# Passing the hi and lo parts of the activations as one moving operand, with weight blocks of 256 columns, in a two-layer encoder trunk

## The chip, the cores and the metric

The kernel runs on one core of one Trainium2 chip. The metric is the device time of one execution in microseconds; the median of three runs before the change is 2806.14 us (2806.04 to 2807.89). Engines are named as in the profile: PE is TensorE's matmul, PEld its weight load, DVE VectorE, ACT ScalarE, POOL GpSimd, SP SyncE, whose queue issues the DMAs.

## What is computed

A trunk of two layers on 256 tokens of 2048 features, all in float32. The reference, cut to what matters here:

```
for layer in range(2):
    sh1, sc1, g1, sh2, sc2, g2 = split(silu(c) @ mod_w[layer] + mod_b[layer], 6)
    h = rms_norm(x, norm_mix_w[layer]) * (1 + sc1) + sh1
    if layer == 0:                       # gated DeltaNet heads and band attention
        mix = gdn_attn_mixer(h, ab_w_in, ..., ab_w_out)
    else:                                # Mamba-2 SSD: in 2048 -> 10304, out 4096 -> 2048
        mix = mamba2_ssd(h, ssd_w_in, ..., ssd_w_out)
    x = x + g1 * mix
    h = rms_norm(x, norm_mlp_w[layer]) * (1 + sc2) + sh2
    x = x + g2 * (square(relu(h @ mlp_w1[layer])) @ mlp_w2[layer])   # 2048 -> 8192 -> 2048
```

## The kernel before

**Products.** A float32 product is made of three products in float32r. Each operand is split into hi (the float32r rounding) and lo (the rest): weights W into wh and wl, activations into ah and al, and the sum is wh·ah + wh·al + wl·ah. Activations are kept as units, a hi tile and a lo tile of [128, 4 k-tiles, 256 tokens] each. Weights stream through in chunks of 1 MB: 4 k-tiles (512 rows of W) by 512 columns. `loader` (L436) loads a chunk by a DMA on SP's queue into one of 4 raw buffers and splits each half of it: ACT casts wh (L289), DVE subtracts to wl (L290).

`b_item` (L459) makes the products of a chunk feature-major: for each of 4 column tiles and each k-tile three matmuls, each with its own 128x128 weight load and 256 moving columns (tokens):

```
self.mmx(o, wh[:, k, cs], ah[:, ka], st, False)
self.mmx(o, wh[:, k, cs], al[:, ka], False, False)
self.mmx(o, wl[:, k, cs], ah[:, ka], False, sp)
```

I call these three a triple; a chunk has 16. `a_item` (L486) is token-major: the activations are the weights of the array and 512 columns of W move. Matmuls of both come from one helper line, L280.

**PSUM.** The pool `psg` has 4 tiles of one bank. A block of 512 output columns takes two of them, each [128, 2, 256] with two column tiles, and is summed over 4 chunks (K = 2048). `room` (L164) lets a new block begin only when at most one older one still waits for its evacuation.

**Who uses what.** The first mixer's input projection (w_ab) mixes a_items and b_items. b_blocks make: the first mixer's output projection (`out_blocks`, wo_ab, 16 chunks), both MLPs (w1 and w2, 128 chunks a layer), the SSD input projection but for z (48 of 80 chunks of w_ssd; the 32 of z are a_items, `a_block`), and the SSD output projection (wo_ssd, 2 halves of 16 chunks).

**Evacuation.** `residual` (L670): for each column tile one DVE scalar_tensor_tensor, x += g·psum (L677). `relu2` in `mlp` (L1209): for each two column tiles ACT relu (L1214) and square (L1215), then the split by ACT and DVE. `conv` (L684): ACT copies PSUM to a padded buffer (L693) and starts the result (L703), DVE adds three taps a column tile (L709). `ssd_gate` (L1159), `gdn_z` (L934), `norm_unit` (L630) and `split_unit` (L594) write the (hi, lo) units; in `ssd_gate` the last steps are transposes on PE, ACT for hi (L1196) and DVE for lo (L1197).

**Order.** Work is traced in steps: a chunk's products yield four times, and between, `tick` traces steps of waiting evacuations (`fast`), of the mixers' background tasks (`bg`) and of the adaLN modulation (`pump`, DVE products of 2.3 us at L402 on 1 MB loads). Each engine then has its instructions in an order by these priorities and by readiness, fixed when the kernel is built. A chunk is loaded one item ahead of its products. At a layer's norm, `norm` (L652) traces the first two units at once and leaves the others to `fast`. `out_blocks` (L573) takes the last unit's products of its first two blocks after all others of these: that unit is first needed after six chunks.

Of the kernel before, what the change touches and what calls it, by code (L numbers as in the profile page):

```python
# [10 lines left out]
F32 = mybir.dt.float32  # L11
# [14 lines left out]
# blocks of 512 columns of the input projections  # L26
# [3 lines left out]
# columns of the packed vectors  # L30
# [9 lines left out]
class Task:  # L40
    """a generator that traces a piece of work step by step"""
# [34 lines left out]

class Slot:
    """stands for a task to come"""
# [12 lines left out]
class Item:  # L91
    """the products of one weight chunk, in two halves"""
# [5 lines left out]
class Trunk:  # L98
    """Float32 products run as three single-pass float32r products of operands
    split exactly into hi + lo; activations are kept as (hi, lo) units  # L100
    [128, 4 k-tiles, 256 tokens], weights stream through in chunks of
    [128, 4 k-tiles, 512 columns]. The products of the mixers are traced in
    steps between those of the projections."""

    def __init__(self, tc, ctx, ins, out):
# [9 lines left out]
        self.ps_g = pool("psg", 4, space=PSUM)  # L115
# [32 lines left out]
    def pg(self, shape=None):  # L148
        return self.ps_g.tile(shape or [P, 2, SEQ], F32, tag="g", name=self.nm("pg"))

# [6 lines left out]
    def evac(self, gen, frees=10000):  # L157
        """a task that frees a block's PSUM with its first steps"""
# [5 lines left out]
    def room(self):  # L164
        """at most one block in PSUM waits when another begins"""
# [59 lines left out]
    def drain(self, src=None):  # L225
        """all the products up to here; the next chunk's load may go before"""
# [8 lines left out]
    def rsqrt(self, v, n, tag="rs"):  # L235
        """1/sqrt(v) of a [128, n] tile of positive values, by Newton steps."""
# [13 lines left out]
    def softplus(self, v, n, tag):  # L250
        """max(v, 0) + log1p(exp(-|v|)), log1p(u) = 2 atanh(u / (2 + u))."""
# [18 lines left out]
    def priority(self, d):  # L270
        """trace as if d instructions later"""
# [23 lines left out]
    def bc(self, col, n=P):  # L295
        """[128, k] -> [128, k, n] by broadcast"""
# [6 lines left out]
    def constants(self):  # L303
# [13 lines left out]
        # silu(c) along the free axis of every partition  # L317
# [46 lines left out]
        # blocks below the diagonal that join pairs of s-blocks  # L364
# [8 lines left out]
        # the pairs of single rows, transposed  # L373
# [8 lines left out]
    def mod_start(self, layer):  # L382
        """the vectors of a layer, in the order of their use"""
# [32 lines left out]
    def need(self, v, key):  # L416
        """the rest of a modulation vector"""
# [8 lines left out]
    def pump(self, n=None):  # L426
        """as many half chunks of the modulation as are due"""
# [8 lines left out]
    def loader(self, src, whole=False):  # L436
        """loads a packed chunk; gives [(hi, lo)] for its two pairs of k-tiles"""
# [6 lines left out]
        def load():  # L444
            raw = self.raw_p.tile([P, 4, 512], F32, tag="raw", name=self.nm("raw"))
            nc.sync.dma_start(raw.rearrange("p k c -> p (k c)"), src)
            for hf in range(2):
                if whole:
# [1041 lines left out]
```

## Time and profile before

| | |
|---|---|
| median of 3 runs | 2806.14 us |
| lowest, highest | 2806.04, 2807.89 us |
| profiled execution, span (first to last instruction) | 2810.5 us |
| profiled execution, own time beside the span | not listed; the span is used |
| mean granted TensorE clock | 0.994 |
| instructions | 50778, of them 21300 matmuls |

The profile is one execution, apart from the three runs. Busy time is the time in which an engine had an instruction under way; matmuls overlap, so their mean duration (284 ns for 256 columns) is not the distance from one to the next, which is read from start times in the timeline. A row of the chain of waits gives a piece of the path that ended last; a row of the table by stretches gives each engine's busy time and count in that stretch.

### The profile page before, as it was taken

The page shows a single profiled execution, that of the slowest core. Times are in us where ns is not written, and L with a number is a line of the kernel's source. Part 1 is how long each engine was busy: PE and PEld are TensorE (multiplying, and loading weights), DVE is VectorE, ACT ScalarE, POOL GpSimd, SP SyncE. Part 2 cuts the span into 40 slices and gives each one's busy share as a digit, 9 for nine tenths or more (in the row PEclk, how much of TensorE's full clock was granted, in tenths as well). Part 3 has the DMA queues.
Part 4 walks back from the last instruction along what each step waited for, and adds up shares of the span by engine and source line. Part 5 has one row for each costly group of instructions (what it writes and reads, how often), then busy time and mean ns, then how long its engine had stood idle before and what let it go on. Part 6 is the DMA issues. An engine that isn't in the chain of part 4 may idle for free.

```text
span 2810.5 us, 50778 instructions
## 1 busy us (share of the span) xinstructions
PE 2750.8 (98%) x21300; PEld 2661.0 (95%) x21300; DVE 2008.5 (71%) x2820; ACT 1354.7 (48%) x2033; POOL 23.2 (1%) x96
## 2 busy tenths in 40 slices
PE   5999999999999999999999999999999999999999
PEld 5887989999999999999998899988999999999999
DVE  7898898887766666666888976888774444445454
ACT  3444454444344354454568644676445344354442
POOL 1000000000000000000000000000000000000000
PEclk9999999999999999999999999999999999999999
DMA  9895487868877777776565666656655555555553
GB/s 347 330 331 219 165 314 258 303 246 340 307 288 275 270 270 273 277 277 238 209 228 193 247 242 241 223 189 245 241 185 199 187 180 180 182 186 187 180 188 128
DMA packets 96517, 672.32 MB, mean 239 GB/s; under 512 B 12576, under 2 KB 13600, under 8 KB 15392
## 3 DMA queue, kind: packets, MB, share of 16 engines
q1 hardware_dynamic: 96144, 669.07, 65.0%
q8 instruction: 167, 2.74, 0.4%
q14 instruction: 62, 0.51, 0.1%
q10 hardware_dynamic: 144, 0.01, 0.0%
HBM read 666.94 MB, written 2.10 MB: 238 GB/s over the span
## 4 chain that ended last, share of the span: by engine, by line
PE 93%; DVE 5%; ACT 1%; issue 1%; DMA 0%; SPq 0%; DVEq 0%; ACTq 0%
PE pg L280 85%; PE pm L283 4%; PE pm L280 3%; PE pm L286 1%; DVE wl L290 1%; DVE mraw L402 1%; DVE hf L643 0%; DVE u L645 0%; DVE u L1294 0%; DMA mraw<-in_mod_dram 0%; ACT pm L767 0%; DMA x<-in_x_dram 0%; ACT wh L289 0%; ACT u L644 0%; ACT pg L969 0%
## 5 line engine op out<-in xcount | busy, mean ns | idle before, releaser
L280 PE MATMUL pg<-u,wh 128*128 128x256 f32 x11936 | 2165.1, 284 | 3.6 <-ACT u L644 3.4
L280 PEld LDWEIGHTS pg<-u,wh 128*128 128x128 f32 x11936 | 1867.8, 192 | 8.4 <-ACT u L644 4.6
L280 PE MATMUL pg<-u,wl 128*128 128x256 f32 x5968 | 1690.3, 284 | 3.3 <-DVE wl L290 3.2
L290 DVE TENSOR_TENSOR wl<-raw,wh 128x1024 fp32r<-128x1024 f32 x870 | 1059.6, 1223 | 647.3 <-ACT wh L289 642.7
L289 ACT CAST wh<-raw 128x1024 fp32r<-128x1024 f32 x870 | 907.4, 1048 | 1141.1 <-PE pg L280 995.1
L280 PEld LDWEIGHTS pg<-u,wl 128*128 128x128 f32 x5968 | 1146.8, 192 | 5.6 <-DVE wl L290 5.3
L402 DVE SCALAR_TENSOR_TENSOR mraw<-mraw,crow 128x2048 f32<-128x2048 f32 x192 | 438.6, 2285 | 15.9 <-DMA mraw<-in_mod_dram 15.8
L280 PE MATMUL pg<-wh,u 128*128 128x512 f32 x864 | 282.4, 398 | 0.0
L280 PEld LDWEIGHTS pg<-wh,u 128*128 128x128 f32 x864 | 161.5, 188 | 32.6 <-issue 1.0
L280 PE MATMUL pg<-wl,u 128*128 128x512 f32 x432 | 170.3, 394 | 0.5 <-DVE wl L290 0.3
L280 PEld LDWEIGHTS pg<-wl,u 128*128 128x128 f32 x432 | 81.3, 188 | 18.2 <-DVE wl L290 2.2
L709 DVE SCALAR_TENSOR_TENSOR u<-pad,cst,u 128x256 f32<-128x256 f32 x216 | 92.6, 479 | 2.1 <-ACT u L703 1.3
L677 DVE SCALAR_TENSOR_TENSOR x<-pg,mod,x 128x256 f32<-128x256 f32 x176 | 73.6, 477 | 16.6 <-PE pg L280 16.6
L290 DVE TENSOR_TENSOR u<-rl,u 128x512 fp32r<-128x512 f32 x64 | 44.1, 691 | 45.6 <-ACT u L289 45.5
L280 PE MATMUL pm<-u,wh 128*128 128x256 f32 x256 | 49.0, 295 | 19.5 <-ACT wh L289 19.5
L280 PEld LDWEIGHTS pm<-u,wh 128*128 128x128 f32 x256 | 42.2, 204 | 20.5 <-ACT wh L289 20.3
L644 ACT ACTIVATE u<-hf,mod 128x256 fp32r<-128x256 f32 x64 | 29.6, 502 | 63.0 <-DVE hf L643 63.0
L1214 ACT ACTIVATE rl<-pg 128x512 f32<-128x512 f32 x64 | 38.0, 595 | 30.3 <-PE pg L280 30.3
L1215 ACT ACTIVATE rl<-rl 128x512 f32<-128x512 f32 x64 | 40.5, 632 | 1.9
L1103 ACT ACTIVATE sau<-Umask,sd_Ah 128x128 fp32r<-128x128 f32 x128 | 41.0, 403 | 0.0
L1103 ACT ACTIVATE sau<-Umask,sd_Al 128x128 fp32r<-128x128 f32 x128 | 40.9, 401 | 0.0
L289 ACT CAST u<-rl 128x512 fp32r<-128x512 f32 x64 | 39.7, 620 | 2.0
(266 smaller groups left out, 1306.2 us busy)
## 6 DMA issues: line engine op xcount, KB each, us to landing
raw<-in_w_dram SPq DMA_DIRECT2D x256, 1024.0 KB, 4.8
mraw<-in_mod_dram SPq DMA_DIRECT2D x192, 1024.0 KB, 5.1
raw<-in_w_ssd_dram SPq DMA_DIRECT2D x80, 1024.0 KB, 4.8
raw<-in_w_ab_dram SPq DMA_DIRECT2D x56, 1024.0 KB, 5.3
raw<-in_wo_ssd_dram SPq DMA_DIRECT2D x32, 1024.0 KB, 4.8
raw<-in_wo_ab_dram SPq DMA_DIRECT2D x16, 1024.0 KB, 5.2
x<-in_x_dram SPq DMA_DIRECT2D x4, 512.0 KB, 5.1
out_dram<-x SPq DMA_DIRECT2D x8, 256.0 KB, 2.0
```

What stands on the lines that cost most here:

```text
L280: self.nc.tensor.matmul(o, a, b, start=start, stop=stop, skip_group_check=True)
L283: self.nc.tensor.matmul(o, lhsT, rhs, start=True, stop=True, skip_group_check=True)
L286: self.nc.tensor.transpose(o, a, self.ident[:k, :k])
L289: a = self.nc.scalar.copy(hi, src)
L290: b = self.nc.vector.tensor_tensor(lo, src, hi.bitcast(F32), op=ALU.subtract)
L402: x = nc.vector.scalar_tensor_tensor(raw, raw, 1.0, self.crow, op0=ALU.mult, op1=ALU.mult, accum_out=t[:, f : f + 1])
L644: nc.scalar.activation(hi[:, ff], h[:, f], AF.Identity, bias=shift[:, col])
L677: nc.vector.scalar_tensor_tensor(x[:, ff], ps[b][:, f], g[:, cb * 4 + ff : cb * 4 + ff + 1], x[:, ff], op0=ALU.mult, op1=ALU.add)
L709: nc.vector.scalar_tensor_tensor(h, pad[:, f, 1 + q : 257 + q], w[:, q, j : j + 1], h, op0=ALU.mult, op1=ALU.add)
L1103: nc.scalar.activation(au[:, h], self.U, AF.Copy, scale=A[:, t, hd : hd + 1].bitcast(F32))
L1214: nc.scalar.activation(rl, ps[b], AF.Relu)
L1215: nc.scalar.activation(rl, rl, AF.Square)
```

## The change

hi and lo lie side by side: a unit is now a pair of tiles [128, 2 k-tiles, 2 (hi, lo), 256]. A new `c_item` runs one matmul of 512 moving columns (hi and lo) for wh and one of 256 (hi) for wl; the latter is added to the lo columns, so that a column tile has two sums in its bank, [hi·wh | lo·wh + hi·wl], and the evacuation adds them. Chunks for it hold 8 k-tiles by 256 columns (1 MB as before); a block is 256 columns, two chunks for K = 2048. `psg` becomes 2 tiles of two banks. The first mixer's input projection and the SSD's z keep `b_item` and `a_item` (on halves of the new PSUM tiles). Core of the diff:

```diff
-        self.ps_g = pool("psg", 4, space=PSUM)
+        self.ps_g = pool("psg", 2, space=PSUM)
...
+    def pair(self):
+        return [self.unit(F32R, [P, 2, 2, SEQ]) for _ in range(2)]
...
+    def pw(self):
+        return self.ps_g.tile([P, 2, 2, SEQ], F32, tag="g", name=self.nm("pw"))
...
+    def c_item(self, ps, src, act, first, last, after=None):
+        load, ws = self.loader(src)
+        def run():
+            o_ = ps()
+            for hf, (wh, wl) in enumerate(self.tiles(ws, 256)):
+                for ct in range(2):
+                    o = o_[:, ct]
+                    cs = slice(ct * P, ct * P + P)
+                    for k in range(4):
+                        u = act(2 * hf + k // 2)[:, k % 2]
+                        st = first and hf == k == 0
+                        sp = last and hf == 1 and k == 3
+                        self.mmx(o.rearrange("p a t -> p (a t)"), wh[:, k, cs], u.rearrange("p a t -> p (a t)"), st, sp)
+                        self.mmx(o[:, 1], wl[:, k, cs], u[:, 0], False, sp)
+                    yield
...
+    def c_blocks(self, w, cbs, acts, then, r0=0):
...
+        for r in range(2):
+            for cb in cbs:
+                after = (lambda cb=cb: then(ps[cb], cb)) if r else None
+                self.c_item((lambda cb=cb: get(cb)), w[r0 + r, cb], (lambda n, r=r: acts(4 * r + n)), r == 0, r == 1, after)
...
-        seq = [(cb, n) for cb in (0, 1) for n in order[:3]] + [(0, order[3]), (1, order[3])]
-        seq += [(cb, n) for cb in (2, 3) for n in order]
+        seq = [(0, 0), (1, 0), (0, 1), (1, 1)] + [(cb, r) for cb in range(2, 8) for r in range(2)]
...
     def residual(self, ps, cb, key, last, final=False):
...
+        g, x, b = self.mod[2, key], self.x[cb // 2], cb % 2
+        for f in range(2):
+            for n in range(2):
+                nc.vector.scalar_tensor_tensor(x[:, 2 * b + f], ps[:, f, n], g[:, 2 * cb + f : 2 * cb + f + 1], x[:, 2 * b + f], op0=ALU.mult, op1=ALU.add)
...
+    def conv_wide(self, ps, dst, b, tiles, w, bias):
...
+        nc.scalar.copy(th, ps[:, :, 1])
+        nc.vector.tensor_tensor(pad[:, :, 4:], ps[:, :, 0], th, op=ALU.add)
+        for f in range(2):
+            j = tiles + 2 * b + f
+            nc.scalar.activation(dst[:, 2 * b + f], pad[:, f, 4:], AF.Identity, scale=w[:, 3, j : j + 1], bias=bias[:, j : j + 1])
...
         def relu2(ps):
-            hi, lo = self.unit(F32R), self.unit(F32R)
...
+            p = self.unit(F32R, [P, 2, 2, SEQ])
+            lo = self.s2([P, 2, SEQ], tag="rs")
+            nc.scalar.copy(lo, ps[:, :, 1])
+            nc.vector.tensor_tensor(lo, ps[:, :, 0], lo, op=ALU.add)
+            yield
+            rl = self.s2([P, 2, SEQ], tag="rl")
+            nc.scalar.activation(rl, lo, AF.Relu)
+            nc.scalar.activation(rl, rl, AF.Square)
+            self.split(rl, p[:, :, 0], p[:, :, 1])
...
-            for cb in range(4):
-                self.b_block(w1, f * 4 + cb, acts, lambda ps, a=a: a.append(self.evac(relu2(ps))))
+            for cbs in ((f * 8, f * 8 + 1), *((f * 8 + cb,) for cb in range(2, 8))):
+                self.c_blocks(w1, cbs, half, lambda ps, cb, a=a: a.append(self.evac(relu2(ps), 1)))
```

The first two blocks of each w1 group, and of the first SSD block, have their chunks interleaved (`cbs` with two entries). `norm` gives out a unit on demand, tracing it to its end if it isn't yet. The packing on the host follows: w1, w2, wo_ab, wo_ssd and the non-z part of w_ssd in chunks of 256 columns, z of w_ssd as an input of its own.

## Rows read from the trace of the kernel before

**Rows 1.** The profile page's head, its busy times by engine (busy us, share of the span, instructions) and its chain of work that ended last, by engine and by line.

```profile
span 2810.5 us, 50778 instructions
...
PE 2750.8 (98%) x21300; PEld 2661.0 (95%) x21300; DVE 2008.5 (71%) x2820; ACT 1354.7 (48%) x2033; POOL 23.2 (1%) x96
...
PE 93%; DVE 5%; ACT 1%; issue 1%; DMA 0%; SPq 0%; DVEq 0%; ACTq 0%
PE pg L280 85%; PE pm L283 4%; PE pm L280 3%; PE pm L286 1%; DVE wl L290 1%; DVE mraw L402 1%; DVE hf L643 0%; DVE u L645 0%; DVE u L1294 0%; DMA mraw<-in_mod_dram 0%; ACT pm L767 0%; DMA x<-in_x_dram 0%; ACT wh L289 0%; ACT u L644 0%; ACT pg L969 0%
```

**Rows 2.** The table by stretches: from:to us, length, then busy us (and instructions) of PE, PEld, DVE, ACT and POOL, the granted clock, the DMA engines' busy share and GB/s. In order: the rest of the first mixer's input projection; the first MLP norm with the MLP's start; the first MLP; the SSD norm; the first half of the SSD's input projection; the second half; the second MLP.

```profile
204.00:498.70 294.70, 290.16 (x1880) 254.70 (x1879) 261.71 (x557) 146.68 (x382) 13.88 (x38) 0.99 0.66 241
...
590.80:612.00 21.20, 17.20 (x124) 16.29 (x122) 18.22 (x48) 11.74 (x24) 0.00 (x0) 0.84 0.18 65
612.00:1338.70 726.70, 725.99 (x6046) 725.58 (x6047) 506.43 (x516) 321.48 (x357) 0.00 (x0) 1.00 0.76 282
1338.70:1353.30 14.60, 11.15 (x76) 10.32 (x74) 11.61 (x35) 6.97 (x15) 0.00 (x0) 0.77 0.05 19
1353.30:1631.00 277.70, 277.53 (x1923) 257.03 (x1924) 249.01 (x430) 181.55 (x343) 1.24 (x12) 1.00 0.63 230
...
1792.00:1967.00 175.00, 175.00 (x1071) 154.75 (x1070) 154.27 (x279) 125.91 (x262) 0.41 (x4) 1.00 0.59 212
...
2066.00:2806.40 740.40, 740.29 (x6144) 740.03 (x6144) 375.40 (x385) 326.71 (x367) 0.00 (x0) 1.00 0.52 182
```

**Rows 3.** The table by stretches again (same columns), for three short ones: in the first mixer, at the start of the first MLP and of the SSD projection.

```profile
120.00:150.00 30.00, 28.10 (x182) 24.88 (x181) 29.80 (x39) 10.22 (x12) 0.00 (x0) 1.00 0.90 325
...
600.00:640.00 40.00, 39.39 (x322) 39.04 (x322) 38.33 (x52) 23.61 (x33) 0.00 (x0) 0.99 0.71 273
...
1360.00:1380.00 20.00, 20.00 (x169) 20.00 (x168) 19.58 (x29) 12.49 (x18) 0.21 (x2) 1.00 0.69 242
```

**Rows 4.** The timeline of PE (start us, us, engine, line, operation, out<-in, shape, count): the same place of a triple in the first MLP, 73 triples apart; and the same place of three 512-column matmuls in the z blocks, 17 threes apart.

```profile
899.73 0.40 PE L280 MATMUL pg<-u,wh 128*128 128x256 f32 x2
...
926.01 0.40 PE L280 MATMUL pg<-u,wh 128*128 128x256 f32 x2
...
1941.52 0.39 PE L280 MATMUL pg<-wl,u 128*128 128x512 f32 x1
...
1953.08 0.39 PE L280 MATMUL pg<-wl,u 128*128 128x512 f32 x1
```

**Rows 5.** The profile page's DMA issues: tile<-tensor, queue, operation, count, KB each, median us to landing.

```profile
raw<-in_w_dram SPq DMA_DIRECT2D x256, 1024.0 KB, 4.8
...
raw<-in_w_ssd_dram SPq DMA_DIRECT2D x80, 1024.0 KB, 4.8
...
raw<-in_wo_ssd_dram SPq DMA_DIRECT2D x32, 1024.0 KB, 4.8
raw<-in_wo_ab_dram SPq DMA_DIRECT2D x16, 1024.0 KB, 5.2
```

**Rows 6.** The timeline of PE where a 256-column matmul is followed by 512-column ones (first mixer), and where the unsplit float32 matmuls of 256 columns run (18 of them, and what follows).

```profile
77.10 0.28 PE L280 MATMUL pg<-u,wl 128*128 128x256 f32 x1
77.22 0.40 PE L280 MATMUL pg<-wh,u 128*128 128x512 f32 x1
77.46 0.40 PE L280 MATMUL pg<-wl,u 128*128 128x512 f32 x1
77.69 0.62 PE L280 MATMUL pg<-wh,u 128*128 128x512 f32 x2
...
272.04 4.05 PE L280 MATMUL pg<-hw,raw 128*128 128x256 f32 x18
275.93 0.60 PE L286 MATMUL pm<-ident,aq 128*128 128x128 f32 x4
```

**Rows 7.** Groups by line: line, engine, operation, out<-in with shapes, count, busy us, mean ns, and the idle time before them with what ended it.

```profile
L402 DVE SCALAR_TENSOR_TENSOR mraw<-mraw,crow 128x2048 f32<-128x2048 f32 x192 | 438.6, 2285 | 15.9 <-DMA mraw<-in_mod_dram 15.8
...
L677 DVE SCALAR_TENSOR_TENSOR x<-pg,mod,x 128x256 f32<-128x256 f32 x176 | 73.6, 477 | 16.6 <-PE pg L280 16.6
...
L1294 DVE TENSOR_TENSOR u<-pg,u 128x512 f32<-128x512 f32 x24 | 16.5, 686 | 6.9 <-PE pg L280 6.6
...
L693 ACT COPY pad<-pg 128x512 f32<-128x512 f32 x24 | 14.1, 590 | 6.3 <-PE pg L280 6.3
```

**Rows 8.** The timeline after the first MLP norm: PE's first projection matmuls, and DVE's lo parts of unit 0 (three, then the fourth) and the last of unit 1.

```profile
597.03 1.16 PE L280 MATMUL pg<-u,wh 128*128 128x256 f32 x3 [1.17 <-ACT u L644]
597.07 1.27 DVE L645 SCALAR_TENSOR_TENSOR u<-hf,mod,u 128x256 fp32r<-128x256 f32 x3
...
599.31 0.49 DVE L645 SCALAR_TENSOR_TENSOR u<-hf,mod,u 128x256 fp32r<-128x256 f32 x1 [0.57 <-ACT u L644]
...
603.27 0.48 DVE L645 SCALAR_TENSOR_TENSOR u<-hf,mod,u 128x256 fp32r<-128x256 f32 x1
```

**Rows 9.** The chain of waits in order of time (start us, us, engine, out, line, count): the sums of squares that follow the last matmul of the SSD output projection, and the second MLP.

```profile
2059.90 2.14 PE pm L280 x20
...
2066.11 740.39 PE pg L280 x6144
```

**Rows 10.** The instructions of line 1197, the lo parts that the SSD gates write: count, ns least/median/most, first to last start, forms.

```profile
L1197 DVE SCALAR_TENSOR_TENSOR u<-pm,cst,u x32: 476/480/486, 1561.8 to 1987.8; 128x256 fp32r<-128x256 f32 x32
```

More of the change, by code (lines that the diff above doesn't have):

```diff
@@ L74, with __init__, done, result @@
     done = False
+class Both:
+    def __init__(self, tasks):
+        self.tasks = tasks
+    @property
+    def done(self):
+        return all(t.done for t in self.tasks)
+    @property
+    def result(self):
+        return self.tasks[0].result
 class Slot:
@@ L457, in loader, with tiles @@
         return load, res
+    @staticmethod
+    def tiles(ws, width):
+        return [[w and w.rearrange("p (k c) -> p k c", c=width) for w in half] for half in ws]
     def b_item(self, ps, src, act, first, last, after=None, whole=False):
@@ L463, in run @@
         def run():
-            o_, (ah, al, x) = ps(), act()
-            for hf in range(2):
-                wh, wl = ws[hf]
+            o_, (u, x) = ps(), act()
+            for hf, (wh, wl) in enumerate(self.tiles(ws, 512)):
                 for ct in range(4):
@@ L490, in run @@
         def run():
-            o_, (ah, al, x) = ps(), act()
-            for hf in range(2):
-                wh, wl = ws[hf]
+            o_, (u, x) = ps(), act()
+            for hf, (wh, wl) in enumerate(self.tiles(ws, 512)):
                 for n in range(4):
@@ L511, in a_item, with get @@
         self.still -= 1
+    def c_item(self, ps, src, act, first, last, after=None):
[13 more added lines that the diff above has]
+                    yield
+        self.emit(Item(load, run, after, self.still > 0))
+        self.still -= 1
+    def c_blocks(self, w, cbs, acts, then, r0=0):
+        ps = {}
+        def get(cb):
+            if cb not in ps:
+                self.room()
+                ps[cb] = self.pw()
+            return ps[cb]
+        for r in range(2):
+            for cb in cbs:
+                after = (lambda cb=cb: then(ps[cb], cb)) if r else None
+                self.c_item((lambda cb=cb: get(cb)), w[r0 + r, cb], (lambda n, r=r: acts(4 * r + n)), r == 0, r == 1, after)
     def n_item(self, src, acts, width, sink):
@@ L565, in get @@
                 self.room()
[L566 removed]
+                ps.extend(self.pg(flat))
             return ps
@@ L633, in norm_unit @@
         scale, shift = self.mod[1, key], self.mod[0, key]
-        hi, lo = self.unit(F32R), self.unit(F32R)
+        p = self.pair()
         x = []
@@ L649, in norm_unit @@
                 yield
-        acts.append((hi, lo, x))
+        acts.append((p, x))
     def norm(self, key):
@@ L666, in norm, with get @@
         self.fast += ts[2:]
-        return lambda n: acts[n]
+        def get(n):
+            while len(acts) <= n:
+                self.fast.pop(0).finish()
+            return acts[n]
+        return get
     def residual(self, ps, cb, key, last, final=False):
@@ L946, in gdn_z @@
         u = task.result
-        hi, lo = self.unit(F32R), self.unit(F32R)
+        p = self.pair()
         for b in range(2):
@@ L1186, in ssd_gate @@
         yield
-        hi, lo = self.unit(F32R), self.unit(F32R)
+        p = self.pair()
         for b in range(2):
@@ L1384, in unit_of, with conv_block, sink @@
             return t.result
-        self.out_blocks(i["wo_ab"], unit_of, 0, lambda ps, cb: self.residual(ps, cb, mix0, True), (0, 2, 3, 1))
+        order = (0, 2, 3, 1)
+        self.out_blocks(i["wo_ab"], lambda n: unit_of(order[n // 2])[0][n % 2], 0, lambda ps, cb: self.residual(ps, cb, mix0, True))
         self.drain(i["w1"][0, 0, 0])
         self.rate = 0.45
-        self.mlp(0, self.norm(("mlp", 0)), i["w_ssd"][0, SB_])
+        self.mlp(0, self.norm(("mlp", 0)), i["w_ssd"][0, 2 * (SB_ - SX)])
         acts = self.norm(("mix", 1))
         w = i["w_ssd"]
-        cv = lambda c0: (lambda ps: put(c0, self.conv(ps, (c0 - SX) * 4, self.sconv, self.sconv_b)))
+        hl = lambda n: acts(n // 2)[0][n % 2]
+        def conv_block(c0, then=None):
+            dst, halves = [], []
+            def sink(ps, _):
+                if not dst:
+                    dst.append(self.unit())
+                halves.append(self.evac(self.conv_wide(ps, dst[0], len(halves), (c0 - SX) * 4, self.sconv, self.sconv_b), 1))
+                if len(halves) == 2:
+                    res[c0] = Both(halves)
+                    if then:
+                        then()
+            n = 2 * (c0 - SX)
+            for cbs in ((n, n + 1),) if c0 == SB_ else ((n,), (n + 1,)):
+                self.c_blocks(w, cbs, hl, sink)
         self.rate = 0.2
```

156 lines of the change are left out of this document (79 added, 77 removed).

## The prediction

> **What bounds the kernel now.** I read the busy times and the chain of waits first, then the table by stretches, then PE's start times. PE is busy 98% of the span and is 93% of the chain, 85% of it the products into pg at L280 [rows 1]: the time is the number of projection matmuls times the distance between them. The stretches say where that holds without a gap: both MLPs and both halves of the SSD's input projection have PE busy for all but 0.7 us of their length at full clock, with DVE at 70% in the first MLP, 51% in the second, and 90% and 88% in the two SSD halves [rows 2]. So PE sets the time, and the SSD stretches are where DVE has least left. The gaps that exist are at the norms, where the granted clock is 0.84 and 0.77 [rows 2], and in the first mixer, where DVE is busy 29.80 of 30 us [rows 3].
>
> The distance between matmuls is the point. In the MLP 73 triples of 256-column matmuls take 926.01 - 899.73 = 26.28 us, 360 ns a triple, 120 ns a matmul. In the z blocks 17 threes of 512 columns take 1953.08 - 1941.52 = 11.56 us, 226.7 ns a matmul [rows 4]. The 256 further columns cost 106.7 ns, 2.4 columns a ns (the 2.4 GHz level), so 256 columns are 106.7 ns and each matmul carries 13.3 ns that belong to the instruction, not to its columns.
>
> **The products.** A triple of 256 + 256 + 256 becomes 512 + 256: the same 768 columns, one matmul and one weight load fewer. From the rows: 226.7 + 120 = 346.7 ns against 360, a gain of 13.3 ns. Chunks concerned: 256 of w1 and w2, 48 of the 80 of w_ssd, 32 and 16 of the output projections [rows 5], 352 chunks of 16 triples, 5632 triples. 5632 x 13.3 ns = 75.1 us. No row shows 512 and 256 in turn many times over. Bounds: a 512 right behind a 256 took 240 ns (77.22 to 77.46), the next 230 [rows 6]. If each pair costs 240 + 120 nothing is gained; more than 75 us is excluded by the two steady distances. I take 75.1, since printed starts are rounded to 10 ns and the steady rows have long counts.
>
> One rule of the Trainium skill speaks against it. First the row: the unsplit float32 matmuls of 256 columns show 18 in 275.93 - 272.04 = 3.89 us, 216 ns each [rows 6]; taken as twice the 106.7 ns of 256 columns, that leaves 2.7 ns for the instruction. The Trainium skill ("TensorE: Matmul & The Clock Gate", Back-to-back issue gap) puts the isolated distance at columns/2.4 GHz plus 2.5 ns; by it a triple would save 2.5 ns, and the products 5632 x 2.5 = 14 us as an estimate. The float32 row agrees with that figure, the float32r rows, which are those that change, do not: 120 and 226.7 both leave 13.3.
>
> **What the change adds, and what hides it.** Residual: four scalar_tensor_tensor a 256-column block in place of two: L677's 73.6 us of DVE double [rows 7]. relu2: one ACT copy (0.59, as L693) and one DVE add from PSUM (0.686, as L1294) for each of 64 half blocks [rows 7], 38 us of ACT and 44 of DVE. conv_wide: the copy stays, 24 DVE adds are new, 16.5 us. DVE goes from 2008.5 to 2143 us, 78% of the new time; in the first MLP from 506 to 506 + 22 + 27 = 555 of some 700. DMA moves the same bytes in the same chunks: 282 GB/s in the first MLP [rows 2] become about 292, and the first mixer runs at 325 [rows 3]. SP's queue issues the same number of loads and 8 stores. So all of it is beside PE on average; what follows is where the cover is thin. What is late next is DVE in each case.
>
> *First mixer.* Its products stay, but psg's tiles are two-bank: both halves of a block come free together. The block after next then waits for the second half's evacuation where it waited for the first's, up to 0.69 us (L1294) [rows 7] for each of 18 partial blocks: 0 to 12 us. A changed order can also win a little, down to -3. DVE is full there [rows 3] and gets nothing new, so I take 3.
>
> *Norms (three).* The first matmul now needs hi and lo. It started at 597.03, on hi alone; the first lo is written about 597.6, the fourth of unit 0 at 599.80, the last of unit 1 at 603.75 [rows 8]. The new order uses all of unit 0 by the fourth pair and unit 1 from the ninth on. Walking it at the low clock's distance: start 597.6, four pairs done at about 600.5 (waiting for 599.80), eight at 602.5, unit 1 by 604.1, the chunk by 605.5, against some 604.8 for the same work before (16 triples from 597.03 and about 2 us at the low clock, which I take as the same in both). 0.7 us, and a wait for DVE's next wl: 1.3 a norm, 4 in all; bounds 0 and 3 a norm.
>
> *SSD output, second half.* The last gate's unit was needed after six chunks, 34.6 us; now after two and a half, 13.9. The half begins 768 matmuls of 120 ns before 2059.90 [rows 9], at 1967.7, so the unit is needed at 1981.6; its last lo part began at 1987.8 and took 0.48 [rows 10]. Bounds 0 and 6.7. Being traced earlier, it is hurried, and its last steps still need PE, ACT and DVE in turn: I take 3. In the first half a whole further block lies between, and the first mixer's output needs its last unit no earlier than it is ready: nothing.
>
> *SSD input.* 12 and 10 adds of 0.686 come to stretches where DVE is at 249 of 277.7 and 154 of 175 us [rows 2], while PE wants to be 5 and 4 us faster: 94% in both. A short stretch is already at 19.58 of 20 us [rows 3]. Bounds: 0, or all 16.5 us of the adds. On average there is room, in bursts not: 5.
>
> *MLPs.* At the start of the first, DVE is at 38.33 of 40 us [rows 3]; three relu2 adds, 2 us. At each of 8 borders from w1 to w2 the last relu2 has 9.0 us (one chunk, half the next and two pairs) for a chain of six operations of about 3.8 us behind queued splits: 2 in all. Together 4; bounds 0 and 10.
>
> A block's evacuation itself (four times 0.48 us) has the whole next block, 11.1 us, before its banks are wanted; I cost it at nothing, with DVE's queue as the cover: if DVE ran 9 us behind, every block would pay.
>
> **Sum.** -75.1 + 3 + 4 + 3 + 5 + 4 = -56. The profiled span 2810.5 would become 2754; it lies 4.4 us above the median of the runs, 2806.1, and no other time of that execution is given, so I set the difference against the median: 2750 us. With the lower bounds -78, 2728; with the upper ones -75 + 12 + 9 + 6.7 + 16.5 + 10 = -21, 2785.
>
> **Rivals.**
> 1. *Nothing new shows.* All covers hold; 2806 - 75 = 2731. For it: PE has hardly a gap in the MLPs, and a block's evacuation has 11 us of cover. Against: DVE at 94%. Chance 0.14.
> 2. *DVE's bursts.* The doubled residual and the adds arrive together with splits and the 2.3 us modulation products [rows 7], and evacuation holds up the two-bank tiles: twice my losses and more, 38 to 56 us, 2769 to 2787. For it: the SSD halves and the 19.58 of 20 [rows 3]. Against: 555 of 700 us in the MLP. Chance 0.17.
> 3. *The hand-over comes back (slower).* In the alternation a 512 behind a 256 always takes the 240 ns of the one row that shows it [rows 6]: a pair costs 360, the 75 us are not won and the 19 us of losses stay, 2825 us. It decides from a pair of 357 ns on (19/5632 = 3.4 ns under 360). For it: that row. Against: the next one is 230, and the steady 226.7. Chance 0.05.
> 4. *Only a small part of the 13.3 ns goes with the instruction.* As in the float32 rows, 2.7 ns, 15 us; 2806 - 15 + 19 = 2810: no change. Chance 0.03. By the Trainium skill's 2.5 ns it would be 2811.
>
> **Chances.** The forecast, 2738 to 2766, has 0.61. The range 2728 to 2785 holds it, rival 1 and most of rival 2: about 8 in 10, allowing for a bound of mine that is wrong. A measurement of this kernel tells from no change about 0.2%, 5.6 us. Faster by more: the forecast and rivals 1 and 2, 0.92, less 0.01 for losses beyond their bounds: 0.91. Within: 0.03. Slower: 0.06.
>
> **What would show it.** In the changed profile: about 5632 matmuls fewer, steady pairs 346 to 347 ns apart in the MLP, the second MLP 27 us shorter (2048 triples), L677's successor at twice its count with PE still unbroken. Wrong if pairs lie 357 ns or more apart, if PE's idle time has DVE's evacuations as releasers in the MLPs, or if the SSD halves get longer than 277.7 and 175 us.

## The result, and the profile after

The changed kernel takes 2768.83 us (median of 4 runs, 2763.02 to 2780.75), the kernel before, beside it, 2806.69 (2806.04 to 2807.89): ratio 0.9871, 95% interval 0.9849 to 0.9893, some 38 us faster. The forecast was 2750 in a range of 2728 to 2785. So the sign and the range held, and the time lies 19 us above the forecast, 3 us outside the 2738 to 2766 that the prediction gave its own case. The changed kernel's runs also spread over 18 us, where those of before lie within 2 here (within 6 in later rounds).

The page after: head, busy times, chain by engine.

```profile
span 2767.4 us, 39822 instructions
...
PE 2698.6 (98%) x15668; PEld 2351.3 (85%) x15668; DVE 2135.9 (77%) x3084; ACT 1390.9 (50%) x2097; POOL 23.1 (1%) x96
...
PE 89%; DVE 8%; ACT 1%; issue 1%; DMA 1%; ACTq 0%; DVEq 0%
```

Against [rows 1]: 21300 - 15668 = 5632 matmuls fewer, the forecast's count, and DVE at 2135.9 us where 2143 was forecast. PE is still busy 98% of the span and is 89% of the chain (93% before); DVE's part of the chain went from 5% to 8%. What went is instructions, not idle time.

The table by stretches after (columns as in [rows 2]): the first MLP norm with the MLP's start, the first MLP, two stretches of the SSD's input, the second MLP. Neither here nor in [rows 2] do the stretches begin and end at the same product as their namesakes, so their lengths are not compared below; lengths of stages go from the first start of a stage's products to its last or to the next stage's first.

```profile
580.00:602.20 22.20, 16.26 (x77) 13.22 (x76) 19.22 (x50) 11.84 (x24) 0.00 (x0) 0.77 0.17 62
602.20:1310.00 707.80, 704.75 (x4043) 618.77 (x4043) 553.49 (x613) 337.37 (x389) 0.00 (x0) 1.00 0.80 291
1320.00:1584.70 264.70, 263.09 (x1433) 223.88 (x1433) 244.78 (x425) 178.21 (x334) 1.24 (x12) 0.99 0.63 224
1754.50:1932.00 177.50, 177.13 (x942) 148.81 (x941) 160.96 (x287) 126.73 (x261) 0.41 (x4) 1.00 0.61 218
2042.60:2763.00 720.40, 719.73 (x4074) 624.08 (x4074) 413.57 (x463) 339.11 (x390) 0.00 (x0) 1.00 0.54 185
```

Read the last row first. In the second MLP PE waits for next to nothing (719.73 of 720.40 us busy) and DVE has time (413.57). The row leaves out the first 22 matmuls, so the whole stage is read from its first and last product:

```profile
2036.46 0.77 PE L307 MATMUL pw<-u,wh 128*128 128x512 f32 x1 [1.84 <-DVE u L710]
...
2762.05 0.28 PE L307 MATMUL pw<-u,wl 128*128 128x256 f32 x1
```

That is 725.6 us, where the 6144 matmuls of before took 740.1 (2066.11 [rows 9] to 2806.20; 739.4 in a second trace): 14 us shorter, and not 27. Next to nothing there is late: the matmuls themselves stand further apart than forecast. The timeline of PE shows it, the same place of a pair 60 pairs apart, in the first MLP and in the second:

```profile
900.03 0.39 PE L307 MATMUL pw<-u,wh 128*128 128x512 f32 x1
...
920.84 0.39 PE L307 MATMUL pw<-u,wh 128*128 128x512 f32 x1
...
2300.01 0.40 PE L307 MATMUL pw<-u,wh 128*128 128x512 f32 x1
...
2321.21 0.40 PE L307 MATMUL pw<-u,wh 128*128 128x512 f32 x1
```

20.81 / 60 = 346.8 ns a pair in the first MLP, as forecast from [rows 4]; 21.20 / 60 = 353.3 ns in the second. Both are steady: the same instructions, at full clock, with no gap. In between, 512 to 256 takes 230.0 ns in the one and 236.7 in the other, 256 to 512 takes 116.7 in both. If all 11264 matmuls of the pairs are set against 226.67 and 120 ns (distances within 25 ns of these; the others are waits or the low clock), the profiled run lost 2.0 ns on each, 22.1 us in all: 13.4 in the second MLP, 5.3 in the SSD, 2.0 in the first MLP, 1.5 in the first mixer's output. I call this the rhythm's cost. It is more than the 19 us that were missing.

My theory: with turns of 512 and 256 PE has two steady distances, 346.7 and 353.3 ns a pair, and which one holds is settled by chance after each interruption. The rival is the forecast's own rival 2: DVE's doubled evacuations hold up PE. A third question was the first mixer, which ended earlier than forecast.

### The profile page after: what moved, and what is told of

The parts are those of the page before. It is cut to its first block, busy times and chain, and to the rows that moved or that the text cites. A ratio compares the mean times of both kernels' runs of the same rounds, so it can differ in the third digit from the quotient of the medians.

```text
span 2767.4 us, 39822 instructions
## 1 busy us (share of the span) xinstructions
PE 2698.6 (98%) x15668; PEld 2351.3 (85%) x15668; DVE 2135.9 (77%) x3084; ACT 1390.9 (50%) x2097; POOL 23.1 (1%) x96
## 4 chain that ended last, share of the span: by engine, by line
PE 89%; DVE 8%; ACT 1%; issue 1%; DMA 1%; ACTq 0%; DVEq 0%
PE pw L307 69%; PE pg L307 11%; PE pm L310 4%; PE pm L307 3%; DVE wl L317 2%; DVE mraw L429 2%; PE pm L313 1%; ACT wh L316 1%; DMA raw<-in_w_ab_dram 1%; DVE x L748 0%; DVE hf L707 0%; DVE u L1390 0%; DVE u L710 0%; ACT pm L861 0%; DVE u L803 0%
## 5 line engine op out<-in xcount | busy, mean ns | idle before, releaser
L307 PE MATMUL pw<-u,wh 128*128 128x512 f32 x5632 | 1993.7, 398 | 9.9 <-DVE u L710 5.5
L307 PE MATMUL pw<-u,wl 128*128 128x256 f32 x5632 | 1583.3, 281 | 1.1 <-DVE wl L317 1.0
L317 DVE TENSOR_TENSOR wl<-raw,wh 128x1024 fp32r<-128x1024 f32 x870 | 1056.8, 1222 | 468.3 <-ACT wh L316 467.2
L307 PEld LDWEIGHTS pw<-u,wh 128*128 128x128 f32 x5632 | 1060.5, 188 | 265.1 <-issue 9.1
L307 PEld LDWEIGHTS pw<-u,wl 128*128 128x128 f32 x5632 | 1067.9, 190 | 4.4 <-DVE wl L317 2.0
L307 PE MATMUL pg<-wh,u 128*128 128x512 f32 x864 | 280.3, 397 | 0.0
L748 DVE SCALAR_TENSOR_TENSOR x<-pw,mod,x 128x256 f32<-128x256 f32 x352 | 161.7, 480 | 67.1 <-PE pw L307 63.9
L307 PEld LDWEIGHTS pg<-wh,u 128*128 128x128 f32 x864 | 161.4, 188 | 32.5 <-issue 0.5
L307 PE MATMUL pg<-wl,u 128*128 128x512 f32 x432 | 170.6, 395 | 0.9 <-DVE wl L317 0.8
L307 PE MATMUL pg<-u,wh 128*128 128x256 f32 x672 | 124.6, 285 | 0.0
L307 PEld LDWEIGHTS pg<-u,wh 128*128 128x128 f32 x672 | 105.7, 192 | 0.3
L307 PEld LDWEIGHTS pg<-wl,u 128*128 128x128 f32 x432 | 81.4, 188 | 17.4 <-DVE wl L317 2.0
L307 PE MATMUL pg<-u,wl 128*128 128x256 f32 x336 | 95.2, 283 | 0.0
L307 PE MATMUL pm<-u,wh 128*128 128x256 f32 x256 | 47.9, 291 | 19.2 <-ACT wh L316 19.2
L307 PEld LDWEIGHTS pg<-u,wl 128*128 128x128 f32 x336 | 64.4, 192 | 0.1
L317 DVE TENSOR_TENSOR u<-rl,u 128x512 fp32r<-128x512 f32 x64 | 44.1, 690 | 20.9 <-ACT u L316 20.9
L307 PEld LDWEIGHTS pm<-u,wh 128*128 128x128 f32 x256 | 41.1, 199 | 20.2 <-ACT wh L316 20.0
L1307 ACT COPY rs<-pw 128x512 f32<-128x512 f32 x64 | 37.1, 579 | 20.2 <-PE pw L307 20.2
```

What stands on the lines that cost most here:

```text
L307: self.nc.tensor.matmul(o, a, b, start=start, stop=stop, skip_group_check=True)
L317: b = self.nc.vector.tensor_tensor(lo, src, hi.bitcast(F32), op=ALU.subtract)
L748: nc.vector.scalar_tensor_tensor(x[:, 2 * b + f], ps[:, f, n], g[:, 2 * cb + f : 2 * cb + f + 1], x[:, 2 * b + f], op0=ALU.mult, op1=ALU.add)
L1307: nc.scalar.copy(lo, ps[:, :, 1])
```

## The experiments

All were timed in three rounds beside the kernel before unless said otherwise (medians of before: 2807.51 for the first four, 2807.66 for the next three, 2807.80 for the last three).

**1. The additions without the gain.** The wide product is taken apart again.

```diff
-self.mmx(o.rearrange("p a t -> p (a t)"), wh[:, k, cs], u.rearrange("p a t -> p (a t)"), st, sp)
+self.mmx(o[:, 0], wh[:, k, cs], u[:, 0], st, sp)
+self.mmx(o[:, 1], wh[:, k, cs], u[:, 1], False, False)
```

> The changed kernel with the 512-column product taken apart again: hi and lo are two products of 256 columns with the same weights, everything else (blocks of 256 weight columns, the two-bank PSUM tiles, the doubled residual, the relu2 and convolution adds) stays. This measures the additions alone. If the forecast's sum is right (the products gain 75 us, the rest costs 19): 2806 + 19 = 2825 us, triples 360 ns apart. If instead the products gain less because a 512 + 256 pair has a second steady distance of 353.3 ns (about 25 us of the 75 lost in the profiled run) and the additions cost little: products gain 50, so 2769 + 50 = about 2819 us, and triples at 360 ns with no second distance. If waits for DVE and ACT eat the gain (55 us of additions): they have more room when PE is slower, so some 2806 + 20 to 2806 + 40, but without a second distance in the steady stretches.

2816.0 us (2815.37 to 2818.2); ratio 1.0032 (1.0020 to 1.0043). The steady place in the two MLPs of this kernel, by stretches of 160 us:

```profile
900.00:1060.00 160.00, 160.00 (x1335) 160.00 (x1335) 116.73 (x128) 76.19 (x88) 0.00 (x0) 1.00 0.76 276
2100.00:2260.00 160.00, 160.00 (x1336) 160.00 (x1335) 90.14 (x103) 73.18 (x82) 0.00 (x0) 1.00 0.54 190
```

1335 and 1336 matmuls in 160 us are 120 ns each, in both MLPs: no second distance with one width. So the additions cost 8.5 us while PE is slow, not 19, and the wide product alone brings 2816.0 - 2768.8 = 47 us, not 75 (net of what the additions cost more with a faster PE). The size of the product term is what was off.

**2. Wide and narrow products in groups of four.** For each 128 columns first wh with k = 0 to 3, then wl with k = 0 to 3.

> The changed kernel with the order of a group's products changed alone: for each 128 columns of a half chunk first the four 512-column products (wh), then the four 256-column ones (wl), where before they came in turn. Same instructions, same operands. Rhythm theory (the second steady distance of 353.3 ns belongs to the turn of 512 and 256, and costs some 25 us of the profiled run): steady groups of four pairs in 1387 to 1400 ns, no stretch at 353.3 a pair, 2745 to 2755 us. Wait theory (the 19 us missing against the forecast are waits for DVE and ACT in the SSD and the MLPs, as rival 2 had it): 2764 to 2772 us, as the changed kernel. If a switch between 512 and 256 costs by itself, fewer switches gain even against 346.7: below 2745.

2772.45 us (2770.09 to 2775.25): no gain. By the number alone this is the wait theory's case, but the trace shows another cause. Four pairs take 1403.3 ns (1400 in one stretch) all through the trace, 350.8 a pair: 234, 234.5, 232 and 228.4 ns for the wide ones, 117.5 to 119.6 for the narrow. So the order of the widths does set the distance, but a row of four does not settle at 226.7. The rhythm costs 21.6 us here by the same count, as in the changed kernel.

**3. DVE relieved.** The sums with lo are left out of every evacuation (their products stay).

```diff
-            for n in range(2):
+            for n in range(1):
...
```

and in the same way in the convolution and in relu2.

> The changed kernel with the lo sums left out of the evacuations (residual: two scalar_tensor_tensor a block and not four; convolution and relu2 read the hi sums straight from PSUM): the products with lo are computed and not used, so part of the sum is missing in the output. DVE and ACT then have about the work of the kernel before: some 135 us of DVE and 38 us of ACT less. Rival 2 (DVE's bursts are where the missing gain is): 19 to 38 us faster than the changed kernel, 2731 to 2750. Rhythm theory: the steady distances stay mixed (346.7 and 353.3), only waits go: about 1 us at each of three norms, 1 at the end, some 5 to 8 in the SSD: 2755 to 2763 us.

2763.55 us (2747.87 to 2764.39): 5.3 us under the changed kernel, half a us above what the rhythm theory gave and far from the 19 to 38 of rival 2. The gaps at the norms, from the last projection matmul to the next, went from 8.1 to 7.1 us and the end from 5.3 to 4.3: 4 of the 5 us. The rhythm was there in full: the whole first MLP at 353.3, the second at 346.7, 21.3 us. One run of this same program took 2747.87, some 16 us less than the three others; it has no trace, so its distances are not known. Rival 2 falls.

**4. Two-bank tiles alone, in the kernel before.**

```diff
-        self.ps_g = pool("psg", 4, space=PSUM)
+        self.ps_g = pool("psg", 2, space=PSUM)
```

with tiles of [128, 2, 2, 256], of which both halves of a block are taken.

> The kernel before with one edit: the four one-bank PSUM tiles of the projection blocks become two two-bank tiles, as in the changed kernel, so both halves of a block come free together. Products, order and evacuations stay. The forecast priced this at +3 us in the first mixer (bounds -3 and +12); the changed kernel reached the end of the first mixer's output 10.8 us earlier, of which only about 2 lie in the output projection itself. If the two-bank tiles make the first mixer faster: 2797 us, with the gain before 490 us of the span. If the order of the tasks (which the whole change moves) or the later norms' work does: 2806 to 2809 us. If the forecast's price is right: 2809.

2815.83 us (2812.84 to 2820.59), 8.3 us slower than before: none of the three numbers. Its trace is read against a second one of before, run 5.

**5. A second trace of the kernel before** (one execution).

> The kernel before, unchanged, for a second trace of it. Its first profiled span, 2810.5 us, lay 4.4 us above the median of the runs, and the changed kernel passed the end of the first mixer's output 10.8 us earlier than that trace. If part of that is the profiled execution's own, this trace ends the first mixer's output some 5 us earlier than 590.5 us, at a span of about 2805; if the change makes the first mixer faster, again at 590.

2807.4 us, span 2805.7, and the first mixer's output ends at 586.51 us where the first trace had 590.5. So 4 us of the 10.8 belonged to that one execution. Against this trace:

- The first mixer's input ends at 494.47 us before, at 487.99 with two-bank tiles alone, and at 485.90 in the changed kernel. It gets 6.5 us shorter by the tiles, where +3 was forecast with -3 as the bound.
- In run 4 it is given back at once: PE waits 4.1 us for DVE's lo part of an activation unit (L291). The timeline of PE there:

```profile
495.14 0.28 PE L281 MATMUL pg<-u,wh 128*128 128x256 f32 x1
499.50 0.39 PE L281 MATMUL pg<-u,wh 128*128 128x256 f32 x1 [4.08 <-DVE u L291]
```

The output projection takes 99.3 us there against 92.0, and ends at 587.24, 0.7 later than before. In the changed kernel the same wait is 0.7 us, and the output ends at 579.73.

- The evacuation of a stage's last block became longer. DVE after the first MLP's last block, at the SSD norm, before (first two rows) and with two-bank tiles (last two):

```profile
1334.50 0.88 DVE L677 SCALAR_TENSOR_TENSOR x<-pg,mod,x 128x256 f32<-128x256 f32 x2 [0.56 <-PE pg L280]
1336.62 0.16 DVE L623 TENSOR_SCALAR nv<-pm 128x2 f32<-128x2 f32 x1 [1.25 <-PE pm L280]
```

```profile
1335.35 1.66 DVE L678 SCALAR_TENSOR_TENSOR x<-pg,mod,x 128x256 f32<-128x256 f32 x4 [3.58 <-PE pg L281]
1338.32 0.16 DVE L624 TENSOR_SCALAR nv<-pm 128x2 f32<-128x2 f32 x1 [1.31 <-PE pm L281]
```

Two operations remain after the last matmul before, four with the tile of both halves, since none starts until the whole tile is written. The norms' gaps go from 6.2, 6.2 and 6.5 us to 7.3, 7.3 and 7.5, and the end from 4.3 to 5.1: 3.9 us together. The SSD is 2.9 us longer (715.1 to 718.0), all of it in the two halves of its input projection.

**6. The order mirrored: 512, 256, 256, 512.**

```diff
+for lo in ((0, 1) if k % 2 == 0 else (1, 0)):
```

with the narrow product where lo is 1, the wide one where it is 0.

> The changed kernel with every second pair's two products in the other order (512, 256, 256, 512), so that the width changes half as often as with strict turns. If each change of width has a price of its own (in groups of four, 16.5 ns on two changes), two pairs with two changes take 2 x 346.7 + 16.5 = 710 ns, 355 a pair: 2806 - 5632 x 5 ns + 8.5 = about 2786 us. If the second distance of 353.3 ns comes from the strict turns of two widths falling into step, and the mirrored order breaks the step: 346.7 to 350 a pair, 2746 to 2765 us, with one distance all through. If the order says nothing: 2765 to 2781, both distances, as the changed kernel.

2759.2 us (2756.22 to 2760.7): the second case. PE in the first and in the second MLP of this kernel, a wide pair and the wide pair of 30 turns later, then two turns of the second MLP:

```profile
900.67 0.63 PE L307 MATMUL pw<-u,wh 128*128 128x512 f32 x2
...
921.57 0.63 PE L307 MATMUL pw<-u,wh 128*128 128x512 f32 x2
...
2300.34 0.63 PE L307 MATMUL pw<-u,wh 128*128 128x512 f32 x2
2300.81 0.39 PE L307 MATMUL pw<-u,wl 128*128 128x256 f32 x2
2301.04 0.62 PE L307 MATMUL pw<-u,wh 128*128 128x512 f32 x2
```

(921.57 - 900.67) / 30 = 696.7 ns for two pairs, 348.3 a pair, and the same in the second MLP (700 ns in printed starts, 696.7 over its whole length). One distance all through, 1.7 ns over the ideal, and the runs lie within 5 us instead of 18. (All kernels without strict turns spread over 1 to 8 us in a round, run 4 the most; those with them over 12 to 27.)

**7. The narrow product into the other half of the tile.**

```diff
-self.mmx(o[:, 1], wl[:, k, cs], u[:, 0], False, sp)
+self.mmx(o[:, 0], wl[:, k, cs], u[:, 0], False, sp)
```

> The changed kernel with the 256-column product (wl with hi) added to the other half of the PSUM tile, the sums with hi, so that it does not write the columns that the 512-column product before it wrote last; the total is the same sum. If the second distance of 353.3 ns comes from adding to columns that were written just before: 346.7 ns all through, about 2746 us. If it comes from the turn of the widths and not from where they write: both distances again, 2763 to 2781 us, as the changed kernel.

2768.0 us (2764.96 to 2777.12), both distances again (first MLP: 346.7 up to some 870 us, 353.3 from there on; second MLP 346.7): where the narrow product writes is not the cause.

**8 and 9. Groups of eight and of sixteen.** For eight, the loop over wh and wl lies outside that over the two 128-column groups of a half chunk; for sixteen, outside both half chunks.

> The changed kernel with eight 512-column products (wh, both 128-column groups of a half chunk) and then the eight 256-column ones. In groups of four the profiled run had 234, 234.5, 232 and 228 ns for the four wide ones (226.7 in long rows) and 117.5 to 119.6 for the narrow ones (120), 16.5 ns a group over the long rows. If that is a price of the change of width which fades with the fourth product, eight pairs take 8 x 346.7 + 16.5 = 2790 ns, 2 ns a pair less than in groups of four: 2772 - 11.5 = about 2761 us. If each wide product after a narrow one costs whatever the group: as groups of four, 2772. Waits for DVE: the low parts of the weights are wanted later, so none of it changes.

2761.23 us (2760.2 to 2761.4), where 2761 was expected. One timeline shows a group, wide and narrow:

```profile
901.11 2.00 PE L307 MATMUL pw<-u,wh 128*128 128x512 f32 x8
902.95 1.11 PE L307 MATMUL pw<-u,wl 128*128 128x256 f32 x8
903.90 2.00 PE L307 MATMUL pw<-u,wh 128*128 128x512 f32 x8
```

2.79 us for eight pairs (2793.3 ns in the mean, everywhere): 233, 236, 228, 232, 231 and then 226.7 for the wide ones, 113, 119 and then 120 for the narrow.

> The changed kernel with a whole chunk's sixteen 512-column products first and then its sixteen 256-column ones. Eight and eight took 2793.3 ns, 20 ns over 8 x 346.7, and the 20 ns lay in the first five wide products and the first two narrow ones, the rest stood at 226.7 and 120. If that is paid once for each way there and back: 16 x 346.7 + 20 = 5567 ns, 347.9 a pair, 1.25 ns a pair less than in eights: 2761 - 7 = about 2754 us, one distance all through and runs within 3 us of each other. If the longer wait for the second half chunk's weights, which must be there before any narrow product, costs PE: 2760 us or more, with PE's gaps at the first wide product of a chunk.

2758.49 us (2757.66 to 2761.76). The group took 5566.6 ns, as expected to the nanosecond, and the rhythm's cost is 7.3 us against 13.9 in eights; but only 3 of those 7 us reach the time. Waits longer than 0.4 us between the matmuls of the pairs add up to 11.1 us in place of 8.2. Most of the further ones come behind the three norms (0.58 us each) and at the SSD's last gate, where sixteen wide products in a row reach the next activation unit sooner and PE waits for DVE's lo part of it (L714, L1296); they are not the waits for weights that the second expectation had in mind.

**10. The changed kernel again.**

> The changed kernel again, unchanged, for a second trace and more runs. If its pairs stand at 346.7 or at 353.3 ns for long stretches by chance: another mix of the two in another trace of the same program, times between about 2746 and 2783 us, a spread of 10 us and more where the kernels with one distance stayed within 5. If the distance is set by the program (by what is computed where): the same stretches at 353.3 as in the first trace, among them the whole second MLP.

2770.43 us (2756.8 to 2783.87, a spread of 27 us). The stretches 900 to 1060 us (first MLP) and 2100 to 2260 us (second), in the first trace of the changed kernel and then in this one:

```profile
900.00:1060.00 160.00, 160.00 (x925) 141.10 (x924) 121.70 (x133) 78.50 (x90) 0.00 (x0) 1.00 0.78 285
2100.00:2260.00 160.00, 160.00 (x908) 138.82 (x907) 90.66 (x102) 73.66 (x83) 0.00 (x0) 1.00 0.54 189
```

```profile
900.00:1060.00 160.00, 160.00 (x907) 138.73 (x906) 119.89 (x133) 77.48 (x89) 0.00 (x0) 1.00 0.76 279
2100.00:2260.00 160.00, 160.00 (x926) 139.92 (x924) 91.37 (x102) 74.51 (x83) 0.00 (x0) 1.00 0.54 191
```

The number of matmuls in the same 160 us is 925 and 926 at the one distance (346 ns a pair, but for the edges) and 907 and 908 at the other (353), and the two MLPs have changed places: by exact starts 346.7 and 353.3 in the first trace, 353.3 and 346.7 in this one. The second MLP takes 712.5 us in place of 725.6. It is the same program, at a granted clock of 1.00 in all four rows, and either distance comes with either load of DVE and the DMA engines; so the place in the program does not set it, which is the theory's case. Not every place is open, though: in all four traces with strict turns (two of the changed kernel, runs 3 and 7) 144 us across the middle of the SSD (1606.6 to 1750.8 in the first) stand at 353.3, and some 50 us towards its end (1961.6 to 2011.5) at 346.7. So "by chance" is shown for the MLPs alone, and what settles it is not shown. Over the whole of this trace the rhythm cost 18.1 us.

**11. The mirrored order, and the last block of a stage as before the change.** Three narrow products into one sum for the last block of each output projection and of w2, in two one-bank tiles.

```diff
+if cb not in ps and one:
+    ps[cb] = [self.pm([P, 512])[:, :SEQ] for _ in range(2)]
...
+if one:
+    self.mmx(o, wh[:, k, cs], u[:, 0], st, False)
+    self.mmx(o, wh[:, k, cs], u[:, 1], False, False)
+    self.mmx(o, wl[:, k, cs], u[:, 0], False, sp)
+    continue
```

> The mirrored order (512, 256, 256, 512), and the last block of each stage (output projections, w2) done as before the change: three 256-column products into one sum, in two one-bank PSUM tiles, so that its first half is evacuated while the second is computed and no second scalar_tensor_tensor follows. If the two-bank tile (+1.05 us) and the second scalar_tensor_tensor (+1.0) are what lengthened the norms' gaps from 6.2 to 8.1 us and the end from 4.3 to 5.3: gaps of some 6.2 to 6.8 us, the end 4.3, four last blocks of 32 triples 12 ns longer each (1.5 us): 2759 - 4 = about 2755 us. If the gaps come from the first pair's need of lo: they stay at 8 us, and the time at 2759 or 2760.

2754.74 us (2752.93 to 2756.11), ratio 0.9807 (0.9792 to 0.9823): the fastest of all, 14 us below the changed kernel's median. DVE after the first MLP's last matmul, in the changed kernel and then in this one:

```profile
1309.65 1.91 DVE L748 SCALAR_TENSOR_TENSOR x<-pw,mod,x 128x256 f32<-128x256 f32 x4 [3.40 <-PE pw L307]
1312.70 0.16 DVE L687 TENSOR_SCALAR nv<-pm 128x2 f32<-128x2 f32 x1 [1.15 <-PE pm L307]
```

```profile
1308.88 0.48 DVE L760 SCALAR_TENSOR_TENSOR x<-pm,mod,x 128x256 f32<-128x256 f32 x1 [2.08 <-PE pm L307]
1310.32 0.48 DVE L760 SCALAR_TENSOR_TENSOR x<-pm,mod,x 128x256 f32<-128x256 f32 x1 [0.96 <-PE pm L307]
1311.95 0.16 DVE L699 TENSOR_SCALAR nv<-pm 128x2 f32<-128x2 f32 x1 [1.15 <-PE pm L307]
```

One operation of 0.48 us is left after the last matmul, where four took 1.91. The gaps are 6.7 us at all three norms (8.2 in run 6) and the end 3.8 (5.4).

## Why the prediction was right, and where it was off

Sums are of the profiled run against the second trace of before (spans 2767.4 and 2805.7, -38.3 us), since the first lay 5 us over it.

- **The products: -75.1 forecast, -53.0 measured** (75.1 less the rhythm's 22.1). This is the step that was off: "I take 75.1, since ... the steady rows have long counts". The rows of one width have long counts [rows 4]; that two widths in turn keep the sum of their distances was an assumption, and the prediction said itself that no row shows it. 346.7 does occur, but beside 353.3, and runs 2, 6, 8 and 9 show other orders with distances of their own. The bound was rightly drawn between 0 and 75. Rival 3 took the 240 ns of [rows 6] for the price of each turn (360 a pair); 353.3 is half way to it.
- **First mixer with its output: +3 forecast, -4.8** (-6.8 for the whole, less the 2.0 that 256 pairs gain there). The sign was wrong: with the tiles coming free together the input's matmuls end 6.5 us earlier (run 4). Why they do is not shown; PE has no single wait there that went.
- **Norms: 4 forecast, 5.4** (6.2, 6.2 and 6.5 us before, 8.14, 8.09 and 8.09 after). 0.7 each is the wait for the first lo, as walked through from [rows 8]: from the last transposes to the first matmul 2.53 us in place of 1.6 to 1.8. Run 1 shows it apart: its first product needs hi alone, and its gaps are 7.4, 7.4 and 7.6. The other 1.0 each was costed at nothing: a block's evacuation was given the next block as its cover, and the last block of a stage has none. Run 11 takes it back, and half a us more, since only one of the four is left behind the last matmul. The same 1.0 us stands at the end of the kernel.
- **SSD: 3 + 5 forecast, 7.6.** From the norm to the next norm 715.1 us became 711.0, where 1280 pairs would have gained 17.1 and lost 5.3 to the rhythm. By the same products, the input's two halves went from 268.4 and 260.8 us to 267.2 and 258.9, 3.9 us less of a gain than their 384 pairs each leave after the rhythm. The forecast's 5 was for the convolution's adds; but run 4, without any, has 2.9 of it, and run 3, which leaves them out, is only 1.1 better (267.0 and 258.8 us, with 0.8 more of rhythm). So most of it comes with the two-bank tiles, and the size came out near the forecast for another reason. The second half of the output went from 92.9 to 93.6, 3.6 us over what its 256 pairs leave; run 4 has nothing of it (92.9), run 1 has it (96.6), which fits the last gate's unit being needed sooner, the forecast's 3.
- **MLPs: 4 forecast, 5.4.** All but 0.1 is in the first: 741.4 us became 721.5, 27.3 - 2.0 less than before would be 716.1. More than half of it is one place, the first border from w1 to w2. The timeline of ACT and PE there, in the changed kernel's first trace:

```profile
681.38 0.59 ACT L1307 COPY rs<-pw 128x512 f32<-128x512 f32 x1 [5.66 <-PE pw L307]
681.86 1.99 ACT L316 CAST wh<-raw 128x1024 fp32r<-128x1024 f32 x2
...
682.96 0.51 PE L307 MATMUL pw<-u,wh 128*128 128x512 f32 x1 [1.62 <-ACT wh L316]
684.22 0.39 PE L307 MATMUL pw<-u,wl 128*128 128x256 f32 x1 [0.76 <-DVE wl L317]
```

  ACT casts the next weights right behind relu2's copy of the block that PE has just ended, and PE waits for the cast and then for DVE's wl: two products come 1.8 and 1.0 us late, in both traces of the changed kernel, where the delays at this border add up to 1.2 before. In this trace the matmuls then go at the 1.2 GHz level for a while (granted clock 0.69 from 684.5 to 690 us), 1.6 us more. The forecast had 2 us for all eight borders together.
- **Nothing for the evacuations within a stage: right.** L677's successor has twice the count, and PE waits for it nowhere within the MLPs:

```profile
L748 DVE SCALAR_TENSOR_TENSOR x<-pw,mod,x 128x256 f32<-128x256 f32 x352 | 161.7, 480 | 67.1 <-PE pw L307 63.9
```

  161.7 us against 73.6 [rows 7] and idle for want of PE, not the reverse. Run 3, without half of them, gains only what lies at the norms and the end.

Together: -53.0 - 4.8 + 5.4 + 7.6 + 5.4 + 1.0 = -38.4, the spans' -38.3 but for rounding. The additions came to 14.6 us where 19 were forecast, so the result is the forecast's mechanism with its main term 22.1 us too large. That the additions came out below the forecast is luck: without the first mixer's unforeseen gain they are 19.4 where 16 were forecast. How far inside the range the median fell is luck too: eight runs of the same program took 2756.8 to 2783.87 us, the highest 1 us under the range's end. The time lies at the edge of rival 2's 2769 to 2787, and for another reason: rival 2 wanted DVE's bursts, and runs 1, 3 and 10 show PE's own distance instead. Of the prediction's signs, the 5632 fewer matmuls and the doubled count came, the second MLP 27 us shorter did not (14), and of those of being wrong none came: no steady pair at 357 ns or more, no wait of PE for a residual's evacuation in the MLPs, and by the same products both SSD halves got shorter, by 1.3 and 1.9 us. The 277.7 and 175 us that it set as their marks are lengths of stretches of [rows 2] that are not the halves: the first runs on into the output projection, the second begins well inside its half.

By the Trainium skill's 2.5 ns an instruction ("TensorE: Matmul & The Clock Gate", Back-to-back issue gap) the products would have gained 14 us as an estimate; run 1 against the changed kernel shows 47. Here the measurement decides against the page's figure, as the float32r rows had it.

## What to carry to other kernels

A steady distance read from instructions of one width need not hold for two widths in turn: where such a sequence is new, the range should reach from the ideal sum to the nearest row in which the widths do change, and its order (mirrored, or in long groups) is worth a run by itself. Work that hides behind "the next block" is bare at the last block of a stage, so count the stage ends one by one. A kernel whose runs spread over nearly 1% at full granted clock is asking for its start distances to be compared between two traces of the same program.

## What the hardware showed that was not expected

- Two steady distances of the same two instructions: 346.7 and 353.3 ns for a 512 and a 256 column matmul in turn. Either held for 590 to 700 us on end, and in the four traces with strict turns it changed only where PE was interrupted. Most interruptions change nothing: in the first trace waits of 1.62 and 0.76 us at 683 and 684 us left 353.3 as it was, and one of 0.28 us for DVE's wl was followed by 346.7 (`703.24 0.39 PE L307 MATMUL pw<-u,wl 128*128 128x256 f32 x1 [0.28 <-DVE wl L317]`). 2048 pairs of the second MLP take 725.6 us in the one and 712.5 in the other. What in PE holds it, and what chooses, stays open.
- Other orders of the same products have one distance each, per pair: 348.3 ns mirrored, 350.8 in groups of four, 349.2 in eights, 347.9 in sixteens. After a narrow one it takes five wide products (some 233, 236, 228, 232, 231 ns in groups of eight and sixteen) to come to 226.7, and the first two narrow ones after a wide one are short (113 and 119 ns against 120).
- One-bank PSUM tiles merged into two-bank ones made the first mixer's input 6.5 us shorter, and every stage's end 0.8 to 1.1 us longer.
